# Rounding the squares on ScalarE, queuing background norm sums later, and new groups and orders in a one-core decoder trunk

## The chip, the cores and the metric

The kernel runs on one core of a Trainium2 chip. The metric is the device time of the whole program in microseconds, median of three runs. A core has five instruction streams that matter here: TensorE (PE, the matrix multiplies, with PEld for its weight loads), VectorE (DVE), ScalarE (ACT), GpSimd (POOL, here mostly the issuer of stores), and SyncE (SP, here the issuer of loads). Each stream runs its instructions in the order in which the program lists them and waits, at an instruction, for what other streams and transfers must have delivered.

## The reference

One layer of a decoder trunk in 32-bit floats, on 2064 prompt rows (16 of them meta tokens) and 64 rows of running samples. Cut to what is computed:

```python
h = rmsnorm(x, norm1_g)
z = h @ w_in                      # 1024 -> 5120
a = za * sigmoid(zg)              # first two fifths
a = causal_dwconv(a, width 31)    # per channel
a = layernorm(a + conv_b, ln_g, ln_b)
a = silu(a) @ w_conv_out          # 1024 -> 1024
p = multiscale_pool(zp) @ w_pool * pool_scale
m = sigmoid(gate_a) * a + sigmoid(gate_b) * p
x = x + m @ w_out                 # 1024 -> 1024
h2 = rmsnorm(x, norm2_g)
up = h2 @ w_up                    # 1024 -> 5632
up = causal_dwconv(up, width 3)
x = x + (gelu(g) * v) @ w_down    # 2816 -> 1024
y = rmsnorm(x, final_g)
```

The outputs are y for both groups of rows and the new states of the two convolutions and of the pooling.

## The kernel before

**Layout.** Channels lie on the 128 partitions (8 chunks c = 0..7 of the 1024 channels, KC = 8), rows lie along the free axis. The 2116 rows that are computed are cut into three column blocks b = 0, 1, 2 of 704, 704 and 708 rows. A block is two halves, FIRST and SECOND, of 352 or 354 rows, since one PSUM bank holds 512 numbers per partition.

**Matrix products.** A product in full precision is made from three passes: each operand is split into a rounded part (hi, type fp32r) and a remainder (lo), and `gemm` (line 355) issues lo·hi, hi·lo and hi·hi for each 128x128 weight tile. ACT makes hi by a copy that rounds, DVE makes lo by a subtraction. A unit of the schedule is one output chunk: for `w_out` it has 8 x 3 = 24 matmuls per half, for `w_up` 48 for both halves, for a group of n chunks of `w_down` 3n per half.

**Weights.** A weight is loaded and split once (`raw` to `wb`), written to DRAM in split form (`keep`), and loaded from there (`wb<-keep`) whenever it is used again. There are four `wb` buffers (W_BUFS) and the loader runs up to four weights ahead (LEAD), so a load goes into the buffer of the unit four places earlier, and is issued on SP when that unit's last matmul is done.

**The stages.** For each block: the gates and values of the input projection (G), pooling (PG), the convolution branch's projection (C), the output projection (WO), the feed-forward (FF), in which the down-projection (DN, line 1323) is cut into groups of chunks f of the 22 chunks of the hidden layer: F_GROUPS for blocks 0 and 1, MIX_GROUPS for block 2. Block 2 (MIXED) makes its up-projection from f = 3 on by `pair` (line 991), which forms sums of halves of rows and weights and gets two 48-matmul products from 84 matmuls; to have room for these sums, the running x of block 2 is spilled to DRAM (`xd`) and fetched for each group of DN. A group of DN starts after the first f of the next group; the last one stands at the end, split in FIRST and SECOND. DN adds its products to x on DVE (`add_post`, line 789, a TENSOR_TENSOR s<-s,ps).

**Joined units.** Where a stage waits for a norm, its first units are joined (`join`, line 1147): their matmuls go chunk by chunk over all units of the group, so that chunk 0 of the new h serves three units before chunk 1 is needed. In WO and the last DN (`c + 1 == JOIN`), the first units of FIRST are joined too.

**Norms.** A norm squares the chunks on ACT and adds the squares on DVE (`sumsq`, line 431), both as chunks become ready. Then PE sums over the partitions: 3 (a half) or 6 (a block) matmuls `ps<-s,ones` of 128x1, called the ones below (`ps<-ones,s` in the trace). DVE makes the inverse root from 9 or 10 small instructions on a tile `rs` of 128x3 or 128x6. PE spreads the result over the partitions by 3 or 6 matmuls `ps<-cst,rs`, called the cst below. The LayerNorm also has two matmuls `ps<-s,ones` of 128x352 for the mean (`rsums`, line 379), ahead of these. These matmuls aren't split in hi and lo; the trace has two records for each of them. Each norm is a generator (task); the norms of the second half of WO and of the last DN are on the way of the next matmuls, the others run in the background.

**What sets the order.** The program is written by a planner in Python (`Pace`, and the loop that walks through `units`). It keeps a modelled time at which each engine becomes free and each tile becomes ready. A task is resumed while DVE's modelled time is behind PE's; `yield at(acc)` means that the task goes on only when the model's DVE time has reached the time at which acc is ready. So the place of the ones or the cst in PE's stream depends on how many units were issued when the model reached that time; the hardware then runs the fixed order.

Of the kernel before, what the change touches and what calls it, by code (L numbers as in the profile page):

```python
# [53 lines left out]
PLAIN = 3  # L54
MIX_GROUPS = (6, 6, 5, 5)
MIX_ROOM = 4
# [77 lines left out]
def trunk(ctx: ExitStack, tc: tile.TileContext, A, O):  # L134
# [240 lines left out]

    def at(ap):
        return "at", pace.ready(ap)

# [7 lines left out]

    def rstd_ps(src, n):

        acc = yield from sumsq(src, n)
        yield at(acc)
        halves = 1 if n <= 512 else 2
# [6 lines left out]
        del acc  # L401
        yield at(ps)
        w = mpool.tile([P, 4, 6], F32, tag="rs", name=nm("rs"), bufs=3)
# [9 lines left out]
        stt(m, m, -0.5, v, ALU.mult, ALU.mult)  # L413
        stt(r, m, 1.5, r, ALU.add, ALU.mult)
        for j, (t, c) in enumerate(cuts):
            mm(ps[:, t, c : c + P], w[:, 1, j : j + 1].to_broadcast([P, P]), cst[:, O_ID : O_ID + P], True, True, 4.0)
        yield at(ps)
        return ps[:, :halves, :h]

    def rstd_of(src, n):  # L420
        ps = yield from rstd_ps(src, n)
        yield from room(1)
        out = S(n)
        act(wide(out, ps), ps, AF.Copy)
        yield at(out)
        return out
# [47 lines left out]
    def norm1_first(ts_):  # L474

        c0, c1 = ts_[0] * hx(0), (ts_[-1] + 1) * hx(0)
        xs = [x_load(0, c, c0 - SKIP, c1 - SKIP) for c in range(KC)]
        yield at(xs[0])

        def src(c):  # L480
            yield
            return xs[c]

        r = yield from rstd_of(src, c1 - c0)
        if ts_[0] == 0:
            R["h", 0] = [(S(2 * hx(0), F32R), S(2 * hx(0), F32R)) for _ in range(KC)]

        def first(c):
            stt(xs[c], xs[c], col(O_N1 + c), r, ALU.mult, ALU.mult)
            act(R["h", 0][c][0][:, c0:c1], xs[c], AF.Copy)  # L490
            return xs[c], *(x[:, c0:c1] for x in R["h", 0][c])

        yield from staggered(first)

    def norm1_rstd(b):
        W = WIDTHS[b]
        yield from room(3)
        xs = [x_load(b, c) for c in range(2)]

        def src(c):  # L500
            x = xs.pop(0)
            if c + 2 < KC:
                xs.append(x_load(b, c + 2))
            yield at(x)
            return x

        R["rstd1", b] = yield from rstd_of(src, W)

# [112 lines left out]
    def conv_norm(b):  # L621
# [10 lines left out]
        for c in range(KC):  # L632
# [5 lines left out]
            elif c:  # L638
                tt(acc, acc, cv, ALU.add)
        yield at(acc)  # L640
        ps = rsums(acc, W)
# [13 lines left out]

        ps = yield from rstd_ps(src, W)
        for c in range(KC):
# [131 lines left out]
    def add_post(b, c, ts_, ps, key):  # L789
        x = R["x1", b, c]  # L790
        yield at(x)
        tt(sb(x, b, ts_), sb(x, b, ts_), ps_of(ps, b, ts_), ALU.add)
        if key:
            for t in ts_:
                R[key, b, t] = c + 1
        yield

    def x_part(b, ts_, key):
        c0, c1 = cols(b, ts_)

        def src(c):
            ok = lambda: all(R.get((key, b, t), 0) > c for t in ts_)
            while not ok():
# [305 lines left out]
    def final(b, ts_):  # L1109
        c0, c1 = cols(b, ts_)  # L1110
        r = yield from (rstd_ps if b == NBLK - 1 and ts_[-1] == 1 else rstd_of)(x_part(b, ts_, "x2n"), c1 - c0)
        for c in range(KC):
# [176 lines left out]
    def WO(b, parts):  # L1289
        mark["WO", b] = len(units)  # L1290
        for ts_ in parts:
            for c in range(KC):
                std_unit(
                    W(("out", c), A["w_out"][c]), lambda: R["m", b], b, ts_,
                    lambda ps, c=c, ts_=ts_: add_post(b, c, ts_, ps, "x1n"), (), wait=c == 0,
                    pre=(lambda c=c: x_again(b, c)) if ts_ == parts[0] else None,
                    drop=("m", b) if ts_ == parts[-1] and c == KC - 1 else None,
                )
# [24 lines left out]
    def DN(b, f0, f1, parts=(BOTH,)):  # L1323
        first = len(units)
        for ts_ in parts:
            for c in range(KC):
                def after(ps, c=c, ts_=ts_):
                    yield from add_post(b, c, ts_, ps, "x2n" if f1 == FC else None)
                    if f1 < FC and b in MIXED:
                        spill(b, c)  # L1330
                    if c == KC - 1 and ts_[-1] == 1:
                        for f in range(f0, f1):
                            del R["f", b, f]

                std_unit(
                    W(("dn", c, f0, f1), A["w_dn"][c][:, f0 * P : f1 * P]), lambda: [R["f", b, f] for f in range(f0, f1)],
                    b, ts_, after, (), c == 0, pre=(lambda c=c: fetch(b, c)) if b in MIXED and ts_[0] == 0 else None,
                )
                if f1 == FC and c + 1 == JOIN and ts_ == parts[0]:
                    join(first)  # L1340

    def FF(b, parts, last_parts):
# [283 lines left out]
```

## Time and profile before

| | us |
|---|---|
| median of three runs | 2970.05 |
| the three runs | 2966.85, 2970.05, 2970.11 |
| the profiled execution | 2964.97 |
| its span, first to last instruction | 2963.1 |
| busy: PE | 2913.6 |
| busy: DVE | 2034.2 |
| busy: ACT | 818.3 |
| busy: POOL | 393.9 |

The profiled execution's own time is 1.87 us above its span, and 5.08 us below the median of the runs. The views that the prediction uses are: the waits by releaser (how long an engine stood idle, put down to what ended the wait), the timeline of an engine (start, duration, form, count, and in brackets the idle time ahead of the first instruction of the row, with its releaser), and a table of time windows (busy time of each engine, count of instructions, granted TensorE clock as a fraction of full speed, mean busy share of the 16 DMA engines, and GB/s). Ends of matmuls are modelled, and a per cent or so of their records is missing, so that counts in a timeline are a few short.

### The profile page before, as it was taken

What the parts mean: (1) busy time and instruction counts of PE and PEld (TensorE: products, weight loads), DVE (VectorE), ACT (ScalarE), POOL (GpSimd) and SP (SyncE); (2) the same over time, 40 slices, a digit from 0 to 9 for tenths busy, and PEclk for the clock granted to TensorE, in tenths of its full rate; (3) what the DMA queues carried; (4) which work ended last, traced back from release to release, by engine and by line L of the source; (5) the groups of instructions that cost most, each with busy time, mean ns of one, the idle gap of its engine ahead of it and who ended that gap; (6) DMA issues with size and microseconds to landing.
All of it is one profiled execution on the core that took longest, in us unless ns stands there. A gap on an engine that the chain in (4) does not pass through costs nothing.

```text
span 2963.1 us, 44420 instructions
## 1 busy us (share of the span) xinstructions
PE 2913.6 (98%) x17928; PEld 2906.4 (98%) x17928; DVE 2034.2 (69%) x3007; ACT 818.3 (28%) x1238; POOL 393.9 (13%) x752
## 2 busy tenths in 40 slices
PE   7999999999999999999999999999999999999997
PEld 7999999999999999999999999999999999999997
DVE  7998998679997454743498999655672136544645
ACT  5201334333223232522221212223252113221322
POOL 1111210020010101232110000233320010000000
PEclk9999999999999999999999999999999999999999
DMA  7424554955655655798644344799964375788786
GB/s 278 157 83 163 200 204 169 343 211 176 233 178 201 215 209 189 262 337 292 247 153 150 132 139 144 266 317 320 349 230 150 131 277 185 266 281 272 269 292 241
DMA packets 156780, 660.13 MB, mean 223 GB/s; under 512 B 24992, under 2 KB 31264, under 8 KB 114720
## 3 DMA queue, kind: packets, MB, share of 16 engines
q1 hardware_dynamic: 104112, 416.19, 41.6%
q0 software_dynamic: 52464, 241.11, 20.6%
q8 instruction: 141, 2.31, 0.3%
q14 instruction: 63, 0.52, 0.1%
HBM read 433.17 MB, written 224.05 MB: 222 GB/s over the span
## 4 chain that ended last, share of the span: by engine, by line
PE 71%; DVE 12%; issue 10%; DMA 3%; POOL 2%; ACT 1%; SPq 0%; DVEq 0%; POOLq 0%; ACTq 0%
PE ps L222 71%; DVE s L185 7%; DVE s L181 3%; DVE wb L181 2%; POOL keep L216 2%; DMA wb<-keep 1%; DMA raw<-in_w_up 1%; DMA keep<-s 1%; ACT s L196 1%; DMA keep<-wb 0%; ACT wb L196 0%; POOL raw L210 0%; DMA s<-in_x 0%; SPq L205 0%; DVE rs L185 0%
## 5 line engine op out<-in xcount | busy, mean ns | idle before, releaser
L222 PE MATMUL ps<-s,wb 128*128 128x354 f32 (+3 forms) x17628 | 2879.2, 325 | 18.9 <-ACT s L196 7.6
L222 PEld LDWEIGHTS ps<-s,wb 128*128 128x128 f32 x17628 | 2867.0, 189 | 23.8 <-ACT s L196 8.7
L185 DVE SCALAR_TENSOR_TENSOR s<-s,half,s 128x704 f32<-128x704 f32 (+1 forms) x720 | 619.3, 922 | 0.0
L196 ACT ACTIVATE s<-s 128x704 fp32r<-128x704 f32 (+10 forms) x447 | 313.4, 711 | 765.5 <-DVE s L185 470.2
L181 DVE TENSOR_TENSOR s<-s,s 128x704 fp32r<-128x704 f32 (+11 forms) x526 | 401.1, 775 | 126.2 <-ACT s L196 117.3
L181 DVE TENSOR_TENSOR s<-s,ps 128x704 f32<-128x704 f32 (+4 forms) x225 | 158.4, 715 | 254.0 <-PE ps L222 208.5
L196 ACT ACTIVATE s<-ps 128x356 f32<-128x356 f32 (+6 forms) x197 | 117.3, 601 | 694.3 <-PE ps L222 677.6
L185 DVE SCALAR_TENSOR_TENSOR s<-ps,cst,s 128x704 f32<-128x704 f32 (+1 forms) x188 | 178.2, 949 | 75.8 <-ACT s L196 72.0
L216 POOL DMA_DIRECT2D keep<-s x266 | 142.8, 541 | 563.2 <-ACT s L196 460.8
L185 DVE SCALAR_TENSOR_TENSOR s<-s,cst,s 128x708 f32<-128x708 f32 (+4 forms) x188 | 156.0, 842 | 64.2 <-ACT s L196 58.0
L181 DVE TENSOR_TENSOR wb<-raw,wb 128x1024 fp32r<-128x1024 f32 (+3 forms) x136 | 152.7, 1125 | 39.0 <-ACT wb L196 38.5
L196 ACT ACTIVATE wb<-raw 128x1024 fp32r<-128x1024 f32 (+3 forms) x136 | 132.2, 977 | 155.7 <-PE ps L222 83.7
L216 POOL DMA_DIRECT2D keep<-wb x136 | 77.1, 567 | 700.0 <-DVE wb L181 683.7
L181 DVE TENSOR_TENSOR s<-raw,s 128x512 fp32r<-128x512 f32 x114 | 75.2, 687 | 107.9 <-ACT s L196 89.2
L196 ACT ACTIVATE s<-ps,cst 128x704 f32<-128x704 f32 (+1 forms) x94 | 78.9, 841 | 244.6 <-PE ps L222 235.8
L185 DVE SCALAR_TENSOR_TENSOR s<-s,ps 128x704 f32<-128x704 f32 (+6 forms) x66 | 43.8, 684 | 128.7 <-PE ps L222 117.3
L185 DVE SCALAR_TENSOR_TENSOR s<-s,s 128x704 f32<-128x704 f32 (+2 forms) x96 | 84.8, 886 | 46.2 <-ACT s L196 44.4
L196 ACT ACTIVATE s<-raw 128x512 fp32r<-128x512 f32 x114 | 68.4, 625 | 145.4 <-DMA raw<-in_w_up 122.9
L181 DVE TENSOR_TENSOR s<-s 128x718 f32<-128x718 f32 (+6 forms) x64 | 55.1, 861 | 38.3 <-ACT s L196 32.5
L216 POOL DMA_DIRECT2D out_ffn_s<-sf x44 | 23.6, 537 | 304.4 <-ACT sf L196 257.6
L185 DVE SCALAR_TENSOR_TENSOR sc<-sa,cst,sc 128x64 f32<-128x64 f32 x232 | 47.0, 279 | 1.0 <-ACT sc L196 0.7
L196 ACT ACTIVATE s<-s,half 128x704 f32<-128x704 f32 (+1 forms) x48 | 46.4, 972 | 0.8
(62 smaller groups left out, 480.9 us busy)
## 6 DMA issues: line engine op xcount, KB each, us to landing
wb<-keep SPq DMA_DIRECT2D x227, 1024.0 KB, 4.9
keep<-wb POOLq DMA_DIRECT2D x100, 1024.0 KB, 6.3
keep<-s POOLq DMA_DIRECT2D x266, 256.0 KB, 5.3
wb<-keep SPq DMA_DIRECT2D x40, 640.0 KB, 4.9
wb<-keep SPq DMA_DIRECT2D x32, 768.0 KB, 4.8
raw<-in_w_up SPq DMA_DIRECT2D x44, 512.0 KB, 4.1
raw<-in_w_in SPq DMA_DIRECT2D x40, 512.0 KB, 4.9
raw<-in_w_up POOLq DMA_DIRECT2D x38, 512.0 KB, 8.3
```

The source lines that it names most:

```text
L181: nc.vector.tensor_tensor(out=out, in0=a, in1=b, op=op)
L185: nc.vector.scalar_tensor_tensor(out=out, in0=a, scalar=s, in1=b, op0=op0, op1=op1)
L196: nc.scalar.activation(out, a, func, **kw)
L216: (nc.sync if last else nc.gpsimd).dma_start(out=dst, in_=src)
L222: nc.tensor.matmul(out, lhsT=lhsT, rhs=rhs, start=start, stop=stop, skip_group_check=again)
```

## The change

The change has four parts.

1. In `norm1_first` for block 0, the squares of the SECOND half are no longer made in the SECOND half's own task. The task of FIRST makes each on ACT right behind the rounding of its own chunk, and the SECOND half's task adds them.
2. CALM = 2500 (ns): the norms in the background (`norm1_rstd` of blocks 1 and 2, the LayerNorms `conv_norm` of blocks 1 and 2, the `final` norms of blocks 0 and 1) wait in the planner's model until 2.5 us after their sum, their ones, and in the case of `rstd_ps` their inverse root, are ready. Their matmuls thus come later in PE's stream.
3. TURN = 1: where WO or the last DN runs FIRST and then SECOND, SECOND begins with chunk 7, whose weight FIRST used last and which is not loaded again, and goes on with 0 to 6. The sum of squares of the SECOND half is made in that order too.
4. MIX_GROUPS goes from (6, 6, 5, 5) to (6, 6, 4, 3, 3). In block 2 the last group but one (f = 16, 17, 18) now stands behind the last pair, f = 21, directly ahead of the last group (19, 20, 21). The last group has no joined units, and fetches no x: the group ahead of it leaves x where it is and doesn't spill it.

```diff
-MIX_GROUPS = (6, 6, 5, 5)
+MIX_GROUPS = (6, 6, 4, 3, 3)
+CALM = 2500.0
+TURN = 1
-    def at(ap):
-        return "at", pace.ready(ap)
+    def at(ap, late=0.0):
+        return "at", pace.ready(ap) + late
-    def rstd_ps(src, n):
-        acc = yield from sumsq(src, n)
-        yield at(acc)
+    def rstd_ps(src, n, late=0.0, acc=None):
+        if acc is None:
+            acc = yield from sumsq(src, n)
+        yield at(acc, late)
...
-        yield at(ps)
+        yield at(ps, late)
...
+        if late:
+            yield at(r, late)
...
     def norm1_first(ts_):
-        xs = [x_load(0, c, c0 - SKIP, c1 - SKIP) for c in range(KC)]
+        xs = R["x0", ts_] = [x_load(0, c, c0 - SKIP, c1 - SKIP) for c in range(KC)]
...
-        r = yield from rstd_of(src, c1 - c0)
+        acc = None
+        if ts_ == SECOND:
+            ok = lambda: len(R.get(("q", 0), ())) == KC
+            while not ok():
+                yield "cond", ok
+            qs = R.pop(("q", 0))
+            acc = qs.pop(0)
+            while qs:
+                yield at(acc)
+                tt(acc, acc, qs.pop(0), ALU.add)
+        r = yield from rstd_of(src, c1 - c0, acc=acc)
...
             act(R["h", 0][c][0][:, c0:c1], xs[c], AF.Copy)
+            if ts_ == FIRST:
+                q = S(hx(0))
+                act(q, R["x0", SECOND][c], AF.Square)
+                R.setdefault(("q", 0), []).append(q)
...
-        R["rstd1", b] = yield from rstd_of(src, W)
+        R["rstd1", b] = yield from rstd_of(src, W, CALM)
...
-        yield at(acc)
+        late = CALM if b else 0.0
+        yield at(acc, late)
         ps = rsums(acc, W)
...
-        ps = yield from rstd_ps(src, W)
+        ps = yield from rstd_ps(src, W, late)
...
+    def order_of(ts_):
+        return [*range(KC - 1, KC - 1 - TURN, -1), *range(KC - TURN)] if ts_ == SECOND else list(range(KC))
...
     def WO(b, parts):
+        ws = {}
         for ts_ in parts:
-            for c in range(KC):
+            for c in order_of(ts_):
+                if ts_ != SECOND or c < KC - TURN:
+                    ws[c] = W(("out", c), A["w_out"][c])
...
     def DN(b, f0, f1, parts=(BOTH,)):
-            for c in range(KC):
+            for c in order_of(ts_):
+                if ts_ != SECOND or c < KC - TURN:
+                    ws[c] = W(("dn", c, f0, f1), A["w_dn"][c][:, f0 * P : f1 * P])
...
-                    if f1 < FC and b in MIXED:
+                    if f1 < FC - MIX_GROUPS[-1] and b in MIXED:
                         spill(b, c)
...
-                if f1 == FC and c + 1 == JOIN and ts_ == parts[0]:
+                if f1 == FC and c + 1 == JOIN and ts_ == parts[0] and b not in MIXED:
                     join(first)
...
-                if f == f0 and pend:
+                if f == (f0 if f0 + gs < FC or b not in MIXED else FC - 1) and pend:
                     DN(b, *pend)
```

The changed file has two lines more ahead of the helpers, so that the matmul helper of line 222 is line 224 there, DVE's adding helper 183 for 181, and the load helper 207 for 205.

**Where block 0 goes from WO to FF.** This is PE's stream in the joined group of the first three up-units of the FIRST half (`ps_5509`, `ps_5513` and `ps_5517` before, `ps_5507`, `ps_5511` and `ps_5515` now), which takes nine matmuls for each chunk of h. The ones and cst are those of the norm of WO's SECOND half. Before, the ones stood behind the seventh chunk (`s_5491`) of eight:

```order
L222 MATMUL ps_5517<-s_5491,wb_5427 128x354
L222 MATMUL ps_5582<-ones,s_5238 128x1 x3
L222 MATMUL ps_5509<-s_5499,wb_5361 128x354
L222 MATMUL ps_5509<-s_5500,wb_5361 128x354
L222 MATMUL ps_5509<-s_5499,wb_5361 128x354
L222 MATMUL ps_5513<-s_5499,wb_5393 128x354
L222 MATMUL ps_5513<-s_5500,wb_5393 128x354
L222 MATMUL ps_5513<-s_5499,wb_5393 128x354
L222 MATMUL ps_5517<-s_5499,wb_5427 128x354
L222 MATMUL ps_5517<-s_5500,wb_5427 128x354
L222 MATMUL ps_5517<-s_5499,wb_5427 128x354
L222 MATMUL ps_5582<-cst,rs_5595 128x128 x3
```

Now they stand behind the fifth (`s_5466`), and the cst behind the sixth:

```order
L224 MATMUL ps_5515<-s_5466,wb_5425 128x354
L224 MATMUL ps_5562<-ones,s_5236 128x1 x3
L224 MATMUL ps_5507<-s_5475,wb_5359 128x354
L224 MATMUL ps_5507<-s_5476,wb_5359 128x354
L224 MATMUL ps_5507<-s_5475,wb_5359 128x354
L224 MATMUL ps_5511<-s_5475,wb_5391 128x354
L224 MATMUL ps_5511<-s_5476,wb_5391 128x354
L224 MATMUL ps_5511<-s_5475,wb_5391 128x354
L224 MATMUL ps_5515<-s_5475,wb_5425 128x354
L224 MATMUL ps_5515<-s_5476,wb_5425 128x354
L224 MATMUL ps_5515<-s_5475,wb_5425 128x354
L224 MATMUL ps_5562<-cst,rs_5575 128x128 x3
```

Nine matmuls stand between ones and cst in both; 45 instead of 63 stand ahead of the ones, and 18 instead of none between the cst and the first matmul on the SECOND half's rows.

**The mean of block 1's LayerNorm.** PE's stream in the feed-forward of block 0, while a group of DN with five chunks f is under way (`ps_7843` before; 30 matmuls a unit). `s_4224` is the sum of the eight convolved chunks, and the row with `ones` is `rsums`. Before:

```order
L222 MATMUL ps_7843<-s_7510,wb_7708 128x352
L222 MATMUL ps_7843<-s_7509,wb_7708 128x352 x2
L222 MATMUL ps_7843<-s_7510,wb_7708 128x352
L222 MATMUL ps_7843<-s_7509,wb_7708 128x352
L222 MATMUL ps_7885<-s_4224,ones 128x352 x2
L222 MATMUL ps_7889<-s_6515,wb_7749 128x352
L222 MATMUL ps_7889<-s_6516,wb_7749 128x352
L222 MATMUL ps_7889<-s_6515,wb_7749 128x352 x2
```

Now a further 30-matmul unit of DN and a 48-matmul up-unit (`ps_7922`) are ahead of it:

```order
L224 MATMUL ps_7922<-s_5492,wb_7785 128x354
L224 MATMUL ps_7922<-s_5493,wb_7785 128x354
L224 MATMUL ps_7922<-s_5492,wb_7785 128x354 x2
L224 MATMUL ps_7922<-s_5493,wb_7785 128x354
L224 MATMUL ps_7922<-s_5492,wb_7785 128x354
L224 MATMUL ps_7979<-s_4224,ones 128x352 x2
L224 MATMUL ps_7985<-s_5272,wb_7827 128x354
L224 MATMUL ps_7985<-s_5273,wb_7827 128x354
L224 MATMUL ps_7985<-s_5272,wb_7827 128x354 x2
```

So the two instructions of `rsums` moved behind 78 matmuls that came after them before.

**From the last pair to the last group.** SP's stream of loads. `wb<-keep` with 128x2x640 or 128x2x384 is a weight of a group of DN with five or three chunks f, `s<-xd` is the fetch of x for one chunk c, `sf` a small state. Before, the last pair's weights were followed by those of the last group of five, the first three fetches together:

```order
L205 DMA wb_25868<-keep_19326 128x1024
L205 DMA wb_25910<-keep_6440 128x2x640
L205 DMA sf_25935<-in_st_ffn 128x80
L205 DMA wb_25949<-keep_6507 128x2x640
L205 DMA wb_25963<-keep_6566 128x2x640
L205 DMA s_25995<-xd_0_21936 128x708
L205 DMA s_26001<-xd_1_21952 128x708
L205 DMA s_26007<-xd_2_21960 128x708
L205 DMA wb_26050<-keep_6611 128x2x640
L205 DMA wb_26052<-keep_6660 128x2x640
L205 DMA wb_26054<-keep_6710 128x2x640
L205 DMA s_26058<-xd_3_21977 128x708
```

Now those of DN for f = 16 to 18 follow, with the fetches one by one between them:

```order
L207 DMA wb_25816<-keep_19564 128x1024
L207 DMA wb_25858<-keep_6435 128x2x384
L207 DMA sf_25883<-in_st_ffn 128x80
L207 DMA wb_25897<-keep_6502 128x2x384
L207 DMA wb_25911<-keep_6561 128x2x384
L207 DMA s_25943<-xd_0_21932 128x708
L207 DMA wb_25964<-keep_6606 128x2x384
L207 DMA s_25966<-xd_1_21948 128x708
L207 DMA wb_25987<-keep_6655 128x2x384
L207 DMA s_25990<-xd_2_21956 128x708
L207 DMA wb_26011<-keep_6705 128x2x384
L207 DMA s_26014<-xd_3_21973 128x708
```

The loads are 384 KB instead of 640 KB, and the fetches, whose instructions are the same 354 KB, belong to the last group but one; the last two fetches stand between the first loads of the last group, and of its 15 loads the rest follow without fetches.

More of the change, by code (lines that the diff above doesn't have):

```diff
@@ L418, in rstd_ps, with rstd_of @@
         return ps[:, :halves, :h]
-    def rstd_of(src, n):
-        ps = yield from rstd_ps(src, n)
+    def rstd_of(src, n, late=0.0, acc=None):
+        ps = yield from rstd_ps(src, n, late, acc)
         yield from room(1)
@@ L490, in first @@
             act(R["h", 0][c][0][:, c0:c1], xs[c], AF.Copy)
+            if ts_ == FIRST:
+                q = S(hx(0))
+                act(q, R["x0", SECOND][c], AF.Square)
+                R.setdefault(("q", 0), []).append(q)
             return xs[c], *(x[:, c0:c1] for x in R["h", 0][c])
         yield from staggered(first)
+        del R["x0", ts_]
     def norm1_rstd(b):
@@ L794, in add_post, with src @@
             for t in ts_:
-                R[key, b, t] = c + 1
+                R.setdefault((key, b, t), set()).add(c)
         yield
+    def order_of(ts_):
+        return [*range(KC - 1, KC - 1 - TURN, -1), *range(KC - TURN)] if ts_ == SECOND else list(range(KC))
     def x_part(b, ts_, key):
         c0, c1 = cols(b, ts_)
-        def src(c):
-            ok = lambda: all(R.get((key, b, t), 0) > c for t in ts_)
+        def src(k):
+            c = order_of(ts_)[k]
+            ok = lambda: all(c in R.get((key, b, t), ()) for t in ts_)
             while not ok():
@@ L1110, in final @@
         c0, c1 = cols(b, ts_)
-        r = yield from (rstd_ps if b == NBLK - 1 and ts_[-1] == 1 else rstd_of)(x_part(b, ts_, "x2n"), c1 - c0)
+        last = b == NBLK - 1 and ts_[-1] == 1
+        r = yield from (rstd_ps if last else rstd_of)(x_part(b, ts_, "x2n"), c1 - c0, 0.0 if b == NBLK - 1 else CALM)
         for c in range(KC):
@@ L1290, in WO @@
         mark["WO", b] = len(units)
+        ws = {}
         for ts_ in parts:
-            for c in range(KC):
+            for c in order_of(ts_):
+                if ts_ != SECOND or c < KC - TURN:
+                    ws[c] = W(("out", c), A["w_out"][c])
                 std_unit(
-                    W(("out", c), A["w_out"][c]), lambda: R["m", b], b, ts_,
-                    lambda ps, c=c, ts_=ts_: add_post(b, c, ts_, ps, "x1n"), (), wait=c == 0,
+                    ws[c], lambda: R["m", b], b, ts_,
+                    lambda ps, c=c, ts_=ts_: add_post(b, c, ts_, ps, "x1n"), (), wait=c == order_of(ts_)[0],
                     pre=(lambda c=c: x_again(b, c)) if ts_ == parts[0] else None,
-                    drop=("m", b) if ts_ == parts[-1] and c == KC - 1 else None,
+                    drop=("m", b) if ts_ == parts[-1] and c == order_of(ts_)[-1] else None,
                 )
@@ L1324, in DN @@
         first = len(units)
+        ws = {}
         for ts_ in parts:
-            for c in range(KC):
+            for c in order_of(ts_):
+                if ts_ != SECOND or c < KC - TURN:
+                    ws[c] = W(("dn", c, f0, f1), A["w_dn"][c][:, f0 * P : f1 * P])
                 def after(ps, c=c, ts_=ts_):
                     yield from add_post(b, c, ts_, ps, "x2n" if f1 == FC else None)
-                    if f1 < FC and b in MIXED:
+                    if f1 < FC - MIX_GROUPS[-1] and b in MIXED:
                         spill(b, c)
-                    if c == KC - 1 and ts_[-1] == 1:
+                    if c == order_of(ts_)[-1] and ts_[-1] == 1:
                         for f in range(f0, f1):
@@ L1335, in DN @@
                 std_unit(
-                    W(("dn", c, f0, f1), A["w_dn"][c][:, f0 * P : f1 * P]), lambda: [R["f", b, f] for f in range(f0, f1)],
-                    b, ts_, after, (), c == 0, pre=(lambda c=c: fetch(b, c)) if b in MIXED and ts_[0] == 0 else None,
+                    ws[c], lambda: [R["f", b, f] for f in range(f0, f1)],
+                    b, ts_, after, (), c == order_of(ts_)[0], pre=(lambda c=c: fetch(b, c)) if b in MIXED and ts_[0] == 0 and f1 < FC else None,
                 )
-                if f1 == FC and c + 1 == JOIN and ts_ == parts[0]:
+                if f1 == FC and c + 1 == JOIN and ts_ == parts[0] and b not in MIXED:
                     join(first)
```

## The prediction

> **What bounds the kernel now.** I read PE's busy time first, then the waits of PE by releaser, then PE's timeline for the place of each wait, then windows around these places for the granted clock.
>
> ```profile
> PE 2913.6 (98%) x17928; PEld 2906.4 (98%) x17928; DVE 2034.2 (69%) x3007; ACT 818.3 (28%) x1238; POOL 393.9 (13%) x752
> ```
>
> ```profile
> PE ps L222 <- DVE s L181: 18.0, 6, 9.9
> PE ps L222 <- ACT s L196: 7.6, 4, 2.3
> PE ps L222 <- DVE rs L185: 6.6, 4, 2.0
> PE ps L222 <- DMA wb<-keep: 5.0, 5, 2.5
> PE ps L222 <- issue: 3.8, 1, 3.8
> PE ps L222 <- DVE wb L181: 0.9, 1, 0.9
> ```
>
> PE bounds it: of a span of 2963.1 us it idles 49.5, 41.9 of it in these waits (us, times, longest), the rest behind its last instruction. The change leaves PE's matmuls as they are, so it can win only waits, and what follows them:
>
> ```profile
> 587.30 24.48 PE L222 MATMUL ps<-s,wb 128*128 128x352 f32 x150
> 627.50:634.30 6.80, 6.19 (x20) 5.82 (x21) 6.80 (x15) 3.34 (x7) 6.63 (x8) 0.50 0.00 0
> 2460.40:2467.20 6.80, 6.80 (x28) 6.80 (x27) 1.64 (x10) 0.00 (x0) 0.00 (x0) 0.50 0.20 84
> ```
>
> A matmul takes 24.48/150 = 0.163 us at full clock. In the windows the column before the last two is the granted clock: behind two of the stalls it is 0.50 for about 6.8 us, with 20 and 28 matmuls (x after PE's busy time; the first window holds a short wait) where 6.8/0.163 = 42 go at full clock. A stall here costs its own time and 1.7 to 3.3 us of slow matmuls.
>
> **Part 1, the squares.**
>
> ```profile
> 30.59 0.53 DVE L181 TENSOR_TENSOR s<-s,s 128x358 f32<-128x358 f32 x1 [0.52 <-DVE s L181]
> 34.16 0.72 PE L222 MATMUL ps<-ones,s 128*128 128x1 f32 x6
> 40.32 0.67 PE L222 MATMUL ps<-s,wb 128*128 128x358 f32 x1 [1.77 <-ACT s L196]
> ```
>
> The second half's sum is done at 31.12, and PE, which doesn't wait, takes it at 34.16. Making it earlier saves nothing: the stalls that follow (1.77 in the last row) are the chain behind the ones, which keeps its length. The eight squares only change place on ACT. Covered by the 3.0 us between sum and ones; without that cover a square of some 0.5 us per chunk would be paid. Term: 0, bounds ±0.5.
>
> **Part 3, TURN, at block 0's WO.**
>
> ```profile
> 610.83 0.52 DVE L181 TENSOR_TENSOR s<-s,ps 128x352 f32<-128x352 f32 x1 [1.94 <-PE ps L222]
> 613.21 1.23 DVE L181 TENSOR_TENSOR wb<-raw,wb 128x1024 fp32r<-128x1024 f32 x1 [0.72 <-ACT wb L196]
> 616.21 3.08 DVE L181 TENSOR_TENSOR s<-s,s 128x352 fp32r<-128x352 f32 x6
> 612.63 9.53 PE L222 MATMUL ps<-s,wb 128*128 128x354 f32 x57 [0.85 <-DVE wb L181]
> 621.99 0.72 PE L222 MATMUL ps<-ones,s 128*128 128x1 f32 x6
> 624.76 0.93 PE L222 MATMUL ps<-cst,rs 128*128 128x128 f32 x6 [0.47 <-DVE rs L185]
> 627.50 0.66 PE L222 MATMUL ps<-s,wb 128*128 128x354 f32 x1 [1.81 <-ACT s L196]
> 628.77 11.49 PE L222 MATMUL ps<-s,wb 128*128 128x354 f32 x54 [0.60 <-DVE s L181]
> ```
>
> The last add of WO ends at 611.35, the sum of squares at 619.29; PE takes it at 621.99, behind 63 matmuls of the joined group. Now the ones stand behind 45. The group began at 612.63 - 0.85 - 6 x 0.163 = 610.8, so they come at 610.8 + 45 x 0.163 = 618.1. DVE has between the last add and the sum one weight split (1.2 us), two scalings and one subtraction (0.5 each, as the six in the row at 616.21) less: 619.29 - 2.7 = 616.6, in time. The split of the third weight now precedes the last add, so the 0.85 goes. Between cst and second half stand 18 matmuls, 2.94 us; the chain to hi took 627.50 - 625.69 = 1.81, to lo 628.77 - 625.69 = 3.08, and lo is used one matmul after hi, at 2.94 + 0.16 = 3.10. Both stalls go; the 0.47 stays, and what idles is too little for the clock, whose loss is 11.49 - 54 x 0.163 = 2.7. Term: 0.85 + 1.81 + 0.60 + 2.7 = 6.0, from 3.3 (clock halved all the same) to 6.4.
>
> **TURN at block 2's WO.**
>
> ```profile
> 2453.00:2460.00 7.00, 4.06 (x24) 3.52 (x23) 1.49 (x3) 0.50 (x1) 0.75 (x3) 1.00 1.01 385
> 2456.30 0.73 PE L222 MATMUL ps<-s,wb 128*128 128x356 f32 x3 [0.41 <-DMA wb<-keep]
> 2459.57 3.17 PE L222 MATMUL ps<-s,wb 128*128 128x356 f32 x12 [2.54 <-DMA wb<-keep]
> ```
>
> PE waits 2.95 us for FF's weights, with the DMA engines full (share 1.01, 385 GB/s). The load that TURN drops lay before this stretch and doesn't help; but the spills of x come a unit later, 354 KB x 1.024 / 385 = 0.94 us less ahead of the weights. I take 0.94 and a third of the clock's loss (from 2459.57 to cst's end 7.9 us for work of 4.6, so 3.3): 2.1, from 0 to 6.2.
>
> **Part 2, CALM.** At block 1's LayerNorm:
>
> ```profile
> 365.43 1.34 PE L222 MATMUL ps<-s,ones 128*128 128x352 f32 x4
> 892.12 2.68 PE L222 MATMUL ps<-s,ones 128*128 128x352 f32 x4 [4.72 <-DVE s L181]
> 894.09 22.25 PE L222 MATMUL ps<-s,wb 128*128 128x352 f32 x126
> 890.16 1.81 DVE L181 TENSOR_TENSOR s<-s,s 128x704 f32<-128x704 f32 x2
> 891.89 0.88 DVE L181 TENSOR_TENSOR s<-s,ps 128x704 f32<-128x704 f32 x1
> 820.00:887.00 67.00, 67.00 (x415) 67.00 (x415) 65.07 (x77) 17.20 (x22) 7.04 (x11) 1.00 0.49 176
> ```
>
> PE comes to the mean at 887.40 and DVE has the sum at 891.97. Now 78 matmuls, 12.7 us, stand ahead: PE comes at 887.4 - 6.0 (WO) + 12.7 = 894.1. DVE, busy 65 of 67 us ahead of it, starts this stretch some 3.9 us earlier (the ones) and has two more instructions of 0.88 ahead of the sum: 889.8, or 893.7 if it wins nothing at WO. So the 4.72 goes. The clock's loss is 894.09 + 22.25 - 892.12 = 24.2 for work of 1.34 (at 365, where nothing waits) + 126 x 0.163 = 20.5: 2.3. Term: 7.0, from 0 (the wait comes back whole, rival a) to 7.0. Late next is the LayerNorm itself; in the program's order the rest of block 0's feed-forward stands between it and its user, the convolution branch's projection. The other norms that CALM moves show no wait before (the ones at 365 run through); norm 1 of block 1 becomes later but is covered by the input projection's matmuls: 0.
>
> **Part 4, the groups.**
>
> ```profile
> 2904.74 5.10 PE L222 MATMUL ps<-s,wb 128*128 128x354 f32 x30 [1.59 <-DMA wb<-keep]
> 2912.16 0.43 PE L222 MATMUL ps<-s,wb 128*128 128x354 f32 x1 [2.32 <-ACT s L196]
> 2913.09 22.59 PE L222 MATMUL ps<-s,wb 128*128 128x354 f32 x128 [0.51 <-DVE s L181]
> 2950.99 0.80 PE L222 MATMUL ps<-ones,s 128*128 128x1 f32 x6 [1.80 <-DVE s L181]
> 2953.82 1.65 PE L222 MATMUL ps<-cst,rs 128*128 128x128 f32 x6 [2.04 <-DVE rs L185]
> 2935.50:2951.00 15.50, 13.70 (x90) 13.43 (x88) 11.92 (x31) 3.36 (x7) 0.00 (x0) 1.00 0.64 216
> wb<-keep SPq DMA_DIRECT2D x11, 640.0 KB, 6.1
> wb<-keep SPq DMA_DIRECT2D x2, 640.0 KB, 4.6
> raw<-in_w_dn SPq DMA_DIRECT2D x16, 384.0 KB, 3.6
> ```
>
> (The first DMA row is of the stretch 2903 to 2935, the second of 2935 to 2950.) Behind the last pair PE waits for the last chunk f and for weights; now 144 matmuls of the group 16 to 18, 23.5 us, hide that chain: 1.59 + 2.32 + 0.51 + slow matmuls 22.59 - 128 x 0.163 = 1.7, together 6.1 won. Given back: between ones and cst of the second half stood 15 matmuls (2.45 us), now 9 (1.47), against 2.04 for the root: 0.6. And DVE, busy 11.92 of 15.50 us there, now has the same adds, squares' sums and scalings beside 72 matmuls (11.7 us) instead of 120, so the last sums are later than 1.80 behind PE: 1.0 (0 to 2.5). Weights of 384 KB are issued three units, 3 x 1.467 = 4.4 us, ahead. Their landing is bounded by 3.6 (raw, 384 KB) and 6.1 (640 KB among fetches); nearest is 4.6 for 640 KB in the same place, and less by size: no wait. At a landing L each of 15 units costs L/3 - 1.467: 8.5 in all at 6.1. Net 4.5, from -4 to 6. The group 12 to 15 has 24 instead of 30 matmuls a unit with the same fetch and spill, 1220 KB in 3.9 us or 320 GB/s, below the 385 above, but with the pairs' loads behind it: 0.5 lost, up to 2.
>
> **Sum.** 0 + 6.0 + 2.1 + 7.0 + 4.5 - 0.5 = 19.1. From the profiled execution, 2964.97 (span 2963.1 and 1.87 around it), this gives 2945.9. The median of the runs is 5.08 above that execution; with this the forecast is 2951.0. Part of the scatter may be the one wait that nothing explains, which the change leaves:
>
> ```profile
> 1636.44 8.76 PE L222 MATMUL ps<-s,wb 128*128 128x354 f32 x43 [3.76 <-issue]
> ```
>
> With its slow matmuls (8.76 - 43 x 0.163 = 1.7) it is 5.5, either way.
>
> **Rivals.** (a) DVE sets the pace up to the mean, so what PE wins at WO comes back as the wait at the mean: for it speaks DVE's 65 of 67 us, against it the 12.7 us of matmuls put ahead. The 7.0 is then not won: 2958. (b) The small loads of the last group land as the 640-KB ones did, at 6.1: 8.5 lost, 2959.5. For it: the fetches among the first ones; against it: 384 KB in 1.467 us is 268 GB/s. The Trainium skill ("DMA: Bandwidth & Descriptors") asks in "Bandwidth" for transfers of 1 MiB or more, and so speaks against these loads; its fit of 2.0 us plus bytes at 436 GB/s ("Anatomy of one DMA") would give 2.9 us here, an estimate that leaves no wait. (c) The change doesn't do what it says: both WO places keep their stalls, since the chain behind ones and cst is as long as ever, and the tail gains nothing: only 7.0 less 2 stay, 2965. (d) Slower: the last group's waits for its small loads halve the clock. At landings of 8 us a unit takes 2.67 us of which PE idles 45%; then 144 matmuls take twice 0.163, 23.5 lost (at half speed a unit takes 2.93 and covers its load), and 19.1 - 23.5 gives 2974.5. It decides from landings of some 7 us on, where a third of each unit is idle; the median of the 640-KB loads is 6.1 at its worst. (e) Stalls under 3 us don't halve the clock, something else does, and the slow matmuls at the two WO places and the tail (2.7, 1.1 and 1.7) stay without the stalls: 13.6 won, 2956.5. Against it: 0.50 begins right behind 1.81 with 0.60, and within a us of the end of 2.54; the 1.59 alone is followed by 30 matmuls in 5.10 us, at nearly full speed. The Trainium skill ("TensorE: Matmul & The Clock Gate", "Why this matters for your kernels") sets the limit at gaps of about 3 us; the trace is stricter.
>
> **Chances.** Forecast 0.54, (a) 0.15, (b) 0.13, (c) 0.10, (d) 0.05, (e) 0.03. A measurement of this kernel tells 0.2%, 5.9 us, from no change: below 2964.1 is faster, above 2976.0 slower. Faster: nearly all of the forecast, (a), (b) and (e), a third of (c): 0.83. Slower: half of (d) and some unnamed cost: 0.05. Same: 0.12. The range goes from 2943 (the bounds of WO2 and of the unexplained wait won) to 2963, which takes in (a), (b) and (e).
>
> **What would show it.** In the changed profile: no wait over 1 us from 611 to 630 and none at the mean near 894; clock 1.00 there. The waits by releaser should show "DVE s" near 13 and "ACT s" near 3.5. Behind the last pair no wait, in the second half of the last group one of some 0.6 at cst and one of 2.8 at the last ones. Wrong: waits for `wb<-keep` in the last 25 us, a stall that moved to between 890 and 960, or an unchanged 2.5 at 2459.

## The result

| | before | changed |
|---|---|---|
| median of the runs (us) | 2970.08 | 2946.74 |
| range of the runs (four each) | 2966.85 to 2970.25 | 2944.69 to 2955.86 |
| profiled execution | 2964.97 | 2947.01 |
| its span | 2963.1 | 2945.2 |

The ratio is 0.993 with a 95% interval of 0.9908 to 0.9952: the change makes the kernel faster by 0.7%, 23.3 us between the medians and by 18.0 between the profiled executions. The forecast was 2951.0 in a range of 2943 to 2963.

The waits of PE by releaser in the changed kernel's profile (us, times, longest):

```profile
PE ps L224 <- DVE s L183: 13.6, 3, 9.4
PE ps L224 <- DVE rs L187: 5.6, 5, 2.0
PE ps L224 <- DMA wb<-keep: 5.4, 3, 2.7
PE ps L224 <- issue: 3.8, 1, 3.8
PE ps L224 <- ACT s L198: 3.5, 2, 1.8
PE ps L224 <- DMA cst<-in_cst: 2.2, 1, 2.2
PE ps L224 <- DVE wb L183: 0.4, 1, 0.4
```

The sum is 34.5 us against 41.9 before; "DVE s" fell from 18.0 to 13.6 and "ACT s" from 7.6 to 3.5, as forecast. "DMA wb<-keep" did not fall. PE's timeline shows where (start, duration, form, count, and the wait ahead with its releaser):

```profile
612.21 6.59 PE L224 MATMUL ps<-s,wb 128*128 128x354 f32 x39 [0.42 <-DVE wb L183]
621.41 0.93 PE L224 MATMUL ps<-cst,rs 128*128 128x128 f32 x6 [0.49 <-DVE rs L187]
622.10 270.24 PE L224 MATMUL ps<-s,wb 128*128 128x354 f32 x1674
892.18 1.34 PE L224 MATMUL ps<-s,ones 128*128 128x352 f32 x4
2080.22 81.41 PE L224 MATMUL ps<-s,wb 128*128 128x352 f32 x492 [1.85 <-DMA wb<-keep]
2443.40 0.72 PE L224 MATMUL ps<-s,wb 128*128 128x356 f32 x3 [0.92 <-DMA wb<-keep]
2446.80 3.67 PE L224 MATMUL ps<-s,wb 128*128 128x356 f32 x12 [2.67 <-DMA wb<-keep]
2921.19 0.93 PE L224 MATMUL ps<-cst,rs 128*128 128x128 f32 x6 [0.53 <-DVE rs L187]
2933.39 0.80 PE L224 MATMUL ps<-ones,s 128*128 128x1 f32 x6 [3.68 <-DVE s L183]
```

From the cst of block 0's WO on, 1674 matmuls run without a listed wait to the mean of block 1's LayerNorm, which takes 1.34 us at full clock where it took 2.68 behind a wait of 4.72. Behind the last pair no wait is left until the last cst but one. The table compares the two profiled executions at matmuls that stand at the same count in both programs (in the mean's row, after taking off 78 matmuls of 0.163 us from the changed kernel).

| reached | before | changed | won since the row above |
|---|---|---|---|
| the cst of block 0's WO, first half, done | 587.30 | 587.44 | -0.1 |
| the mean of block 1's LayerNorm, place of before, ahead of its wait | 887.40 | 879.5 | 8.0 |
| the ones at 1440 and 1424 | 1440.43 | 1423.92 | 8.6 |
| the wait for weights near 2080 begins | 2095.02 | 2078.37 | 0.1 |
| the ones of block 2's WO, first half | 2426.64 | 2413.40 | -3.4 |
| the cst of block 2's WO, second half, done | 2467.44 | 2453.75 | 0.5 |
| end of the span | 2963.1 | 2945.2 | 4.2 |

### The profile page after: what moved, and what is told of

The parts are those of the page before. It is cut to its first block, busy times and chain, and to the rows that moved or that the text cites. A ratio compares the mean times of both kernels' runs of the same rounds, so it can differ in the third digit from the quotient of the medians.

```text
span 2945.2 us, 44430 instructions
## 1 busy us (share of the span) xinstructions
PE 2903.2 (99%) x17928; PEld 2896.9 (98%) x17928; DVE 2040.9 (69%) x3015; ACT 817.5 (28%) x1238; POOL 389.2 (13%) x752
## 4 chain that ended last, share of the span: by engine, by line
PE 97%; DMA 1%; DVE 1%; issue 0%; SPq 0%; ACT 0%; DVEq 0%; ACTq 0%
PE ps L224 97%; DMA wb<-keep 1%; DVE s L187 0%; DVE s L183 0%; DMA cst<-in_cst 0%; DMA raw<-in_w_up 0%; SPq L207 0%; ACT s L198 0%; DMA s<-xd 0%; DVE rs L187 0%; DVE rs L183 0%; DVE wb L183 0%; DVE rs L194 0%; ACT wb L198 0%; DVE rs L192 0%
## 5 line engine op out<-in xcount | busy, mean ns | idle before, releaser
L183 DVE TENSOR_TENSOR s<-s,ps 128x704 f32<-128x704 f32 (+4 forms) x233 | 165.2, 720 | 257.9 <-PE ps L224 214.0
```

The source lines that it names most:

```text
L183: nc.vector.tensor_tensor(out=out, in0=a, in1=b, op=op)
```

## The experiments

Times are medians; each kernel was timed beside the kernel before. That one's median was 2965.9 to 2968.6, with single runs from 2960.6 to 2973.2, so a difference of 2 us between two kernels is not told apart by their times alone, and the profiles decide where they can.

### The changed kernel again

> The changed kernel itself, beside the three that follow on the same chip: 2946 to 2947 as before, 20 us under the kernel before.

2947.15 against 2965.87, ratio 0.9938 (0.9925 to 0.995). The change is worth 14.8 to 22.2 us of 2966; in the first measurement, with its 23.3, the runs of the kernel before lay some 4 us high.

### What removes the wait at the mean: TURN or CALM

The changed kernel without CALM:

```diff
-CALM = 2500.0
+CALM = 0.0
```

> The changed kernel with CALM at 0, so that the sums of background norms stand where they stood before. Theory: what TURN won at block 0's WO (8 us between 587 and the mean of block 1's LayerNorm) is won by PE alone, since DVE is the slower one up to the mean; so the wait at the mean comes back larger than before, at 9 to 10 us instead of 4.7, with slow matmuls behind it: some 12 us slower than the changed kernel, 2958. Rival (the parts add up): the wait at the mean is 4.7 again, with 2.5 us of slow matmuls, 2954. If CALM is what made the wait for wb<-keep near 2080 grow from 0.26 to 1.85, that wait is small again, and either time is 3 us lower.

2949.38, ratio 0.9946 (0.9932 to 0.996): both accounts were wrong. PE's timeline of this kernel:

```profile
621.16 0.93 PE L224 MATMUL ps<-cst,rs 128*128 128x128 f32 x6 [0.47 <-DVE rs L187]
621.85 271.50 PE L224 MATMUL ps<-s,wb 128*128 128x354 f32 x1674
893.19 1.34 PE L224 MATMUL ps<-s,ones 128*128 128x352 f32 x4
```

There is no wait at the mean without CALM, and 1674 matmuls stand ahead of it, as many as with CALM. So it isn't CALM that put the mean back by 78 matmuls in the changed kernel. The next runs take each part alone, in the kernel before.

TURN alone (CALM, groups and squares as before):

```diff
+TURN = 1
+    def order_of(ts_):
+        return [*range(KC - 1, KC - 1 - TURN, -1), *range(KC - TURN)] if ts_ == SECOND else list(range(KC))
...
-            for c in range(KC):
+            for c in order_of(ts_):
```

> The kernel before with TURN alone; groups, squares and CALM as before. In the changed kernel without CALM the two matmuls of the mean stood just as far back as with CALM, and had no wait. Theory: it is TURN's new order at block 0's WO that moves the planner past them, so TURN alone wins WO and the mean, 8.1 + 8.5 = 16.6 us: 2951 to 2953. Rival, the prediction's account (CALM moves the mean, TURN only shortens WO): a wait of 4.7 us or more at the mean, and 8 us won or less, 2959 to 2962.

2950.35, ratio 0.9947 (0.9935 to 0.9959), 15.5 us under the kernel before, close to the 16.6 of the theory.

```profile
620.25 0.94 PE L224 MATMUL ps<-cst,rs 128*128 128x128 f32 x6 [0.49 <-DVE rs L187]
620.94 271.77 PE L224 MATMUL ps<-s,wb 128*128 128x354 f32 x1674
892.55 1.35 PE L224 MATMUL ps<-s,ones 128*128 128x352 f32 x4
```

CALM alone:

```diff
+CALM = 2500.0
...
-        yield at(acc)
+        late = CALM if b else 0.0
+        yield at(acc, late)
         ps = rsums(acc, W)
```

> The kernel before with CALM alone. Here CALM moves the mean behind 30 matmuls, 4.9 us, against a wait of 4.72. Theory: the wait at the mean falls to between 0 and 0.8 and its slow matmuls go, all else as before: 7 us won, 2960 to 2963. Rival, both parts are needed at the mean: a wait of 2 us or more, 3 us won or less, 2965.

2959.41, ratio 0.9975 (0.9964 to 0.9985), 6.5 us won where the theory said 7.

```profile
624.17 0.93 PE L224 MATMUL ps<-cst,rs 128*128 128x128 f32 x6 [0.47 <-DVE rs L187]
626.92 0.43 PE L224 MATMUL ps<-s,wb 128*128 128x354 f32 x1 [1.81 <-ACT s L198]
628.18 262.64 PE L224 MATMUL ps<-s,wb 128*128 128x354 f32 x1607 [0.84 <-DVE s L183]
890.66 1.37 PE L224 MATMUL ps<-s,ones 128*128 128x352 f32 x4
```

The waits at WO are all there, the mean is 30 matmuls further back than before (1607 against 1577 in this row) and waits no more. And the changed kernel without TURN:

```diff
-TURN = 1
+TURN = 0
```

> The changed kernel with TURN at 0, so that the second half of WO and of the last DN begins with chunk 0. Theory: between 611 and 630 the waits of about 0.9, 1.8 and 0.6 us come back with half clock behind them, the mean of block 1's LayerNorm stays without a wait, and the stage of block 2's WO changes by less than 1 us: 8 us slower than the changed kernel, 2955. Rival: with CALM in place the order of the second half buys little, since the waits at WO are hidden in what DVE has to do up to the mean: 2947 to 2949.

2955.99, ratio 0.9963 (0.9951 to 0.9976), 8.8 us over the changed kernel.

```profile
628.16 0.66 PE L224 MATMUL ps<-s,wb 128*128 128x354 f32 x1 [1.81 <-ACT s L198]
629.43 262.86 PE L224 MATMUL ps<-s,wb 128*128 128x354 f32 x1607 [0.60 <-DVE s L183]
892.80 1.42 PE L224 MATMUL ps<-s,ones 128*128 128x352 f32 x4 [0.51 <-DVE s L183]
```

The stretch from the cst of WO's first half (the row behind it starts at 587.30 before) to where the unexplained "issue" wait begins, near 1616 to 1633, holds both places and is free of later disturbances. From the profiles it took 1045.4 us before, 1030.6 with TURN alone, 1037.0 with CALM alone, 1028.5 with all, 1030.4 with all but CALM, 1037.5 with all but TURN. TURN alone wins 14.8 of the 16.9, CALM alone 8.4: either removes the wait at the mean, and only TURN removes those at WO. What CALM adds to TURN is 2 us in this stretch and 2.2 in the medians. The other profiles with both parts show 1027.8 to 1028.4 here, but old_squares 1030.2, as without CALM; so whether CALM adds anything to TURN stays open.

TURN moves the mean though it doesn't touch its task. That the planner, whose model sees the second half's norm finished at another unit, takes up the sum of the convolved chunks later is my reading of the program and was not tried.

### The groups

The changed kernel with the groups of before, their place, their joined units and their fetches:

```diff
-MIX_GROUPS = (6, 6, 4, 3, 3)
+MIX_GROUPS = (6, 6, 5, 5)
...
-                if f == (f0 if f0 + gs < FC or b not in MIXED else FC - 1) and pend:
+                if f == f0 and pend:
```

> The changed kernel with the groups 6 6 5 5 of before and the last group but one at its old place. Theory: the waits behind the last pair (1.6, 2.3 and 0.5 us, with 1.7 us of slow matmuls) come back, the wait of 0.5 at the last cst but one goes, and the wait at the last ones falls from 3.7 to 1.8: 4 us slower than the changed kernel, 2951. Rival: the last group's smaller pieces cost on DVE and in loads what they save behind the last pair: 2947, no difference.

2950.56, ratio 0.9943 (0.9931 to 0.9956), 3.4 us over the changed kernel.

```profile
2892.19 5.14 PE L224 MATMUL ps<-s,wb 128*128 128x354 f32 x30 [2.07 <-DVE s L187]
2899.11 0.43 PE L224 MATMUL ps<-s,wb 128*128 128x354 f32 x1 [1.78 <-ACT s L198]
2900.04 4.00 PE L224 MATMUL ps<-s,wb 128*128 128x354 f32 x23 [0.50 <-DVE s L183]
2905.33 19.75 PE L224 MATMUL ps<-s,wb 128*128 128x354 f32 x120 [1.29 <-DMA wb<-keep]
2937.87 0.83 PE L224 MATMUL ps<-ones,s 128*128 128x1 f32 x6 [1.71 <-DVE s L183]
```

The waits behind the last pair are back, and the last ones wait 1.71 instead of 3.68, as expected. The new groups alone, in the kernel before:

```diff
-MIX_GROUPS = (6, 6, 5, 5)
+MIX_GROUPS = (6, 6, 4, 3, 3)
```

(with the lines on the place, joined units, fetches and spills of the change)

> The kernel before with the new groups alone. Theory: the stretch from the last pair on is independent of the rest; the waits of 1.6, 2.3 and 0.5 go, those of 0.5 at the cst and of 3.7 at the last ones come: 4 us faster than before, 2962. The waits at block 0's WO and at the mean are as before. Rival: without TURN the last group's second half starts on a weight that must be loaded again, and the tail gains 2 us or less.

2965.60 against 2966.68, ratio 0.9995 (0.9985 to 1.0005): a gain of 4 us is just inside the interval, no gain too.

```profile
890.02 2.69 PE L224 MATMUL ps<-s,ones 128*128 128x352 f32 x4 [4.83 <-DVE s L183]
1971.53 124.51 PE L224 MATMUL ps<-s,wb 128*128 128x352 f32 x768 [2.80 <-ACT s L198]
2948.90 0.80 PE L224 MATMUL ps<-ones,s 128*128 128x1 f32 x6 [3.68 <-DVE s L183]
```

In the profile the end is as expected, and the wait at the mean is that of before. From the first matmul behind the cst of block 2's WO to the end of the span it takes 492.4 us, against 495.7 before, 491.5 in the changed kernel and 495.0 in old_groups: 3.2 and 3.5 us for the groups in the two pairs. A wait of 2.80 at 1971, which the profiles of the kernel before and of the changed kernel do not have, takes most of that back in this execution.

### The squares

The changed kernel with the second half's squares in their own task:

```diff
-        if ts_ == SECOND:
+        if False:
...
-            if ts_ == FIRST:
+            if False:
                 q = S(hx(0))
                 act(q, R["x0", SECOND][c], AF.Square)
```

> The changed kernel with the squares of the second half in their own task as before. Theory: the sum of the second half is ready 3 us before it is used either way, so the same waits of 2.0, 1.8 and 0.55 us and the same time, 2946 to 2947. Rival: ACT's pairs pace the first matmuls, so without the squares the first matmuls run through faster and it is 1 us faster; or the sum is later and it is 1 us slower.

2947.28, ratio 0.9936 (0.9924 to 0.9948): the same as the changed kernel's 2947.15.

```profile
37.89 0.94 PE L224 MATMUL ps<-cst,rs 128*128 128x128 f32 x6 [2.04 <-DVE rs L187]
40.72 0.67 PE L224 MATMUL ps<-s,wb 128*128 128x358 f32 x1 [1.90 <-ACT s L198]
41.93 25.58 PE L224 MATMUL ps<-s,wb 128*128 128x358 f32 x143 [0.55 <-DVE s L183]
```

The three waits are those of the changed kernel (2.04, 1.77 and 0.55), within 0.13. The stretch from 587 to the "issue" wait is 1030.2 here against 1028.5 in the changed kernel; the times do not show these 2 us, and nothing ties them to the squares.

### What the change leaves: the last ones and block 2's WO

The wait at the last ones grew to 3.68 where 2.8 was forecast. In the changed kernel this is DVE's row ahead of them:

```profile
2930.19 3.06 DVE L183 TENSOR_TENSOR s<-s,s 128x354 f32<-128x354 f32 x5
```

These are five sums of squares in one piece, behind the last add of DN. Listing the last norm's tasks in the other order puts the sums ahead of the scalings of the first half:

```diff
-        for ts_ in SPLIT if b == NBLK - 1 else (BOTH,):
+        for ts_ in (SECOND, FIRST) if b == NBLK - 1 else (BOTH,):
             add_task(("y", b, ts_), final(b, ts_), ...
```

> The changed kernel, with the last norm's tasks listed in the other order, so that DVE adds up the second half's squares ahead of the scalings of the first half's output. Theory: the 3.68 us at the last ones are five adds that queue behind those scalings (3.06 us in one piece); with the adds done as the squares come the wait is about 1.8 and the kernel 1.5 to 2 us faster, 2945. Rival: the wait is the chain of the last chunk (add, square, add) and of the scalings alike; it stays above 3 and the time at 2947.

2944.55, ratio 0.9927 (0.9914 to 0.9939). The wait is 2.27, between the two expectations, and what is left in one piece is two sums, with one scaling (0.58 us at 2930.21) still ahead of them:

```profile
2930.71 1.15 DVE L183 TENSOR_TENSOR s<-s,s 128x354 f32<-128x354 f32 x2
2932.01 0.80 PE L224 MATMUL ps<-ones,s 128*128 128x1 f32 x6 [2.27 <-DVE s L183]
```

At block 2's WO the prediction gave TURN 2.1 us; the waits grew instead, from 2.95 to 3.59. They are 3.80 without TURN, so TURN isn't their cause or cure. In the profiles of all kernels that leave the spills where they were, they scatter from 2.81 to 5.30 with TURN (5.30 in the changed kernel's second profile) and from 2.95 to 3.80 without it. The next kernel, on top of y_swap, issues the eight spills of x together, behind norm 2's last chunk (written here as what it comes to):

```diff
             act(two[0][:, 2:], x, AF.Copy)
-            if t:
-                spill(b, c)
...
         yield from staggered(first)
+        if b in MIXED and ts_[0] == 1:
+            for c in range(KC):
+                spill(b, c)
```

> The changed kernel with the other order of the last norm's tasks (as in y_swap), and with the eight spills of x at block 2's norm 2 issued together, behind its last chunk, instead of one behind each chunk. Theory: the waits for wb<-keep at block 2's WO (0.9 and 2.7 us near 2443, with a dozen matmuls at half speed and 0.5 at the cst behind) come from the DMA engines being full of these spills beside FF's 1024-KB weights; without the spills ahead of them the weights land in 5 instead of 9 us, and the waits fall under 1 us: 4 us faster than y_swap's 2944.6, 2940 to 2941. Rival: the weights alone fill the engines, or the x that stays longer in SBUF holds up the second half's rows: 2944 to 2946, with the wait at the same place or just behind it.

2940.01, ratio 0.9905 (0.9892 to 0.9918). DMA issues in the stretch 2428 to 2445 (count, KB, median us to landing) and a window there (the last three columns are granted clock, DMA share and GB/s), of the changed kernel and then of this one, with PE's row behind the wait:

```profile
wb<-keep SPq DMA_DIRECT2D x4, 1024.0 KB, 9.0
2428.00:2443.00 15.00, 14.48 (x90) 14.19 (x89) 5.69 (x13) 3.13 (x7) 4.47 (x15) 1.00 0.94 349
```

```profile
wb<-keep SPq DMA_DIRECT2D x4, 1024.0 KB, 5.4
2428.00:2442.00 14.00, 13.08 (x82) 12.79 (x80) 4.38 (x9) 2.01 (x4) 5.78 (x17) 1.00 0.78 276
2442.22 2.18 PE L224 MATMUL ps<-s,wb 128*128 128x356 f32 x12 [1.14 <-DMA wb<-keep]
```

The weights land 3.6 us sooner, the waits fall from 3.59 to 1.14, and the twelve matmuls behind run at full clock (2.18 us against 3.67). Against y_swap, which differs in the spills alone, it is 5.4 for 8.6 us to landing and 1.14 for 3.40 us of waits. The spills ahead of the weights are the cause, and 4.5 us are won over y_swap. The stall is not all gone, as expected only roughly ("under 1 us").

A larger last group, also on top of y_swap:

```diff
-MIX_GROUPS = (6, 6, 4, 3, 3)
+MIX_GROUPS = (6, 5, 4, 3, 4)
```

> As y_swap, with the groups 6 5 4 3 4 in place of 6 6 4 3 3, so that the last group has 12 matmuls a unit and 96 in its second half. Theory: DVE keeps up with a second half of 15.7 us; the wait at the last ones falls from 2.3 to 1.8, that at the cst from 0.5 to 0.1, no other wait: 1 us faster than y_swap, 2943.5. Rival: seven chunks of f are live at the last pair instead of six, and the group of three is fetched and loaded while the last pair's weights still come: a wait of 1 us or more behind the last pair, 2945 to 2947.

2944.21 (2939.50 to 2953.36), ratio 0.9921 (0.9907 to 0.9935), no different from y_swap's. The wait at the last ones is 1.80 and there is none at the cst ahead, as expected. The profiled execution happens to be the slowest run, 2953.36, and shows why (PE's timeline, DVE's timeline, and a window):

```profile
2164.76 2.72 PE L224 MATMUL ps<-ones,s 128*128 128x1 f32 x12 [5.19 <-DVE s L183]
2155.46 0.69 DVE L183 TENSOR_TENSOR s<-raw,s 128x512 fp32r<-128x512 f32 x1 [3.18 <-ACT s L198]
2165.00:2172.00 7.00, 7.00 (x28) 7.00 (x29) 3.81 (x6) 2.76 (x5) 3.23 (x6) 0.50 0.72 280
```

A sum of squares in the background, which the edit does not touch, is 5.19 us late, and 7 us at half clock follow. Before it ACT waits, and DVE with it, for a store to DRAM (`keep<-s`) while the DMA engines are full (share 0.98 from 2150 to 2160):

```profile
2154.79 0.63 ACT L198 ACTIVATE s<-raw 128x512 fp32r<-128x512 f32 x1 [4.50 <-DMA keep<-s]
```

By the changed kernel's timelines the same ones come at 2161.47 and do not wait; DVE's sum is ready at 2160.58, 0.9 us ahead.

Both edits together:

> late_spill with the groups 6 5 4 3 4. From the profiles, the stretch from the end of block 2's WO to the end of the program took 499.1 us in y_swap and 497.7 in last_four. Theory: the two edits lie 450 us apart and add up: 1.4 us under late_spill's 2940.0, 2938.6, with waits of about 1.1 at block 2's WO and 1.8 at the last ones. Rival: what last_four wins lies within the scatter of the runs and is not seen, 2940.

2939.40, ratio 0.9908 (0.9891 to 0.9924), against late_spill's 2940.01: the rival's case, a gain too small to see in the times. Its profile shows what was expected:

```profile
2442.76 2.17 PE L224 MATMUL ps<-s,wb 128*128 128x356 f32 x12 [1.06 <-DMA wb<-keep]
2925.81 0.80 PE L224 MATMUL ps<-ones,s 128*128 128x1 f32 x6 [1.80 <-DVE s L183]
```

Late_spill and this kernel both beat the changed kernel, by about 7 us.

## Why the prediction was right, and where not

**The time.** It forecast a gain of 19.1 from profile to profile; 18.0 came. The terms have errors that cancel: the first two stretches won 3.6 us more than their terms, block 2's WO 1.6 less, and 3.4 were lost where nothing was forecast. That the sum came within 1.1 us is in part luck.

**Squares, 0.** Right as far as the times tell: old_squares takes the same, with the same waits.

**TURN at block 0's WO, 6.0.** Right in mechanism: 1.81 and 0.60 are gone, the 0.5 at the cst stayed, the 0.85 fell to 0.42 here (none is listed in turn_only and no_calm). The size was 8.0. Of the 2.0 too little, the term for slow matmuls is the suspect: it was read from 54 matmuls, while the rest of the stretch to the mean is faster too, with no wait listed. The same count of 1674 matmuls took 270.24 us here and 271.77 in turn_only, without a listed wait in either. Over all profiles, the stretch from 587 to the mean's place of before (moved matmuls taken off) takes 299.1 to 300.1 without TURN and 291.4 to 293.1 with it, so that TURN is worth 6.0 to 8.7 by the pair that is compared, and the forecast lies at the low end. Why matmuls without waits differ by half a per cent stays open.

**CALM at the mean, 7.0.** The size was nearly right (8.6), the attribution wrong. The failed step is "Now 78 matmuls stand ahead", put down to CALM: the order of the whole change was read as the effect of the part whose code names this norm. TURN alone moves the mean by the same 78, CALM alone by 30; each is enough. Rival (a), DVE as the pace up to the mean, is seen only in no_turn, as 0.51 us.

**TURN at block 2's WO, 2.1.** Wrong, it was 0.5. The failed step is that the spills come "a unit later" and so are 0.94 us less in the way: the waits were 2.95 before, 3.59 changed and 3.80 without TURN. The 0.5 is within the scatter of this wait. The forecast's own sign of being wrong, an unchanged 2.5, came: 2.67. That the full DMA engines are the limit was right; late_spill shows that the spills must leave the stretch altogether.

**The groups, 4.5 and -0.5.** Right, 4.2 for the stretch (3.2 and 3.5 in the two pairs): no wait behind the last pair, 0.53 at the cst (0.6 forecast). The last ones wait 3.68; the row of five adds gives the 1.9 over before, where 1.0 was taken of a bound of 2.5. Rival (b) did not come: no wait for weights in the last group here, and at most 0.47 in the other kernels with these groups or a last group of four. The DMA issues of the changed kernel between 2893 and 2932:

```profile
wb<-keep SPq DMA_DIRECT2D x15, 384.0 KB, 4.0
```

4.0 us is between the bounds of 3.6 and 6.1, and 0.4 under the 4.4 that the loads have; it is also over the 2.9 of the estimate. Rival (d) needed 7; no run came near, so its threshold is not tested.

**Not forecast.** The wait for weights near 2080 grew from 0.26 to 1.85, with slow matmuls behind it: 3.4 us lost. The other kernels with most of the change show 0.28 to 1.65 at this place and no_turn none, the changed kernel's second profile 1.46; so this is a transfer that lands near the edge and varies from run to run, and I can't say whether the change made it worse.

**The 5.08 from profile to median.** This step failed too: it was taken as belonging to every execution, but was scatter of the kernel before, whose runs spread over 12.6 us. The changed kernel's profiled execution lies at its median. Without it the forecast would have been 2945.9.

**The clock.** Rival (e) is refuted where it matters: with the waits at WO gone, the granted clock between 622 and 640 is 1.00; with them back, in no_turn, it is 0.52. The first row is the changed kernel's, the second no_turn's:

```profile
622.00:640.00 18.00, 18.00 (x114) 18.00 (x113) 17.02 (x27) 7.00 (x12) 8.53 (x18) 1.00 0.18 68
```

```profile
628.20:635.00 6.80, 6.20 (x20) 5.82 (x21) 6.80 (x15) 3.34 (x7) 6.67 (x8) 0.52 0.00 0
```

The limit of about 3 us for a gap ("TensorE: Matmul & The Clock Gate", "Why this matters for your kernels", of the Trainium skill) is thus too mild for this kernel, where waits of 1.81 and 0.60 less than a us apart are enough. That a single wait of 2.80 was not (last section) shows that the length of a gap alone doesn't decide.

## What to carry to other kernels

Where a planner writes the order, an edit moves instructions that it never names; to attribute a moved instruction, look at the order with each part of the change alone, before any run. A stall of two or three microseconds in a stream that is otherwise full cost up to twice its length here, where the clock halved behind it, so it pays to look for what fills the DMA engines ahead of it and can wait: here eight spills. A median of three runs of a kernel whose runs spread by 0.4% is no base for a correction of 0.2%.

## What the runs showed that was not expected

A single wait of 1.85 us, for weights, halved the clock (0.55 from 2081.8 to 2085.2 in the changed kernel), while one of 1.46 at the same place in a second execution of that kernel did not (1.00); and 1.14 in late_spill did not either. Nor did one of 2.80, longer than all of these, in groups_only (third row, right behind it). So the length of a wait alone doesn't tell whether the clock halves; what does is not shown by these runs:

```profile
2081.80:2085.20 3.40, 3.40 (x14) 3.40 (x13) 3.40 (x5) 1.08 (x3) 0.00 (x0) 0.55 0.85 336
```

```profile
2079.70:2086.00 6.30, 6.30 (x39) 6.30 (x40) 6.30 (x9) 2.47 (x4) 0.00 (x0) 1.00 0.73 290
```

```profile
1971.50:1975.00 3.50, 3.47 (x22) 3.50 (x23) 2.98 (x4) 1.30 (x2) 1.61 (x3) 1.00 0.98 369
```

And part of the scatter of these runs is a wait that comes and goes: in last_four's slowest run the ones at 2164.76 waited 5.19 us, with 7 us of half clock behind, which together make the 9 us that this run lies above the others. The same ones wait 1.41 us in old_groups, 1.21 in late_spill and 0.66 in both_tail, and not at all in the changed kernel's two profiles. The 2.80 of groups_only is of the same kind: PE waits for ACT, and ACT for a store `keep<-s` that lands late (2.08 at 1970.20). The changed kernel has single runs of 2955.9 and 2955.2, 9 and 8 us above its medians; that it is the same wait is likely from its 0.9 us of slack there, but no profile caught it at that length.
